# A two-group decoder trunk: weight low parts in two GpSimd operations, and a subtraction of the channel mixer one flush later

## The chip, the cores and the metric

The kernel runs on one core of one Trainium2 chip. The metric is the device time of one execution in microseconds (us), the median of several runs. The engines are called as in the profile: PE is TensorE (matrix products), DVE is VectorE, ACT is ScalarE, POOL is GpSimd, SP is the queue that issues the transfers. "L153" is line 153 of the kernel.

## The reference

One inference step of a decoder of two layers, for two groups of tokens that share one set of weights: a prompt of 1024 tokens and a sample group of 8 sequences with 8 new tokens each (64 tokens, with 1024 cached positions). The width is 1024, the channel mixer's hidden width 2816, everything is float32.

```python
def swiglu(h, w_in, w_out):
    g, u = jnp.split(h @ w_in, 2, axis=-1)
    return (jax.nn.silu(g) * u) @ w_out

for layer in range(DEPTH):
    hn = rms_norm(h, norm_mix_g[layer])
    if layer % 2 == 0:      # convolution module + stick-breaking attention, one in- and one out-projection
        mix = conformer_sb_mixer(hn, ...)
    else:                   # short gated convolution + causal pooling
        mix = shortconv_pool_mixer(hn, ...)
    h = h + mix
    h = h + swiglu(rms_norm(h, norm_ffn_g[layer]), w_ffn_in[layer], w_ffn_out[layer])
y = rms_norm(h, norm_final_g)
```

Outputs are y for both groups, the new keys and values, and the new states of the convolutions and the pooling.

## The kernel before, in words

**High and low parts.** Each float32 operand of a matrix product is used as two numbers: a high part, which is the operand copied to the matrix format, and a low part, which is the operand minus its high part. A product is made of three (`mm3`, L167 to L171): high weight by high operand, high weight by low operand, low weight by high operand, in this order for each 128 rows of the contraction. All run under line L170.

**Weights.** The weights come in 278 tiles of 128 x 1024 numbers, in one fixed list (`seq`). A tile of an input projection holds eight blocks of 128 contraction rows by 128 outputs; a tile of the channel mixer's second matrix holds two blocks of rows by 512 outputs. `w_load` has SP fetch a tile into one of three `stage` buffers. `w_split` has ACT copy the high part (L152) and POOL subtract for the low part (L153) into one of three `hl` buffers. `w_next` hands out a tile, splits those up to two ahead and loads up to five ahead. So the split of a tile waits on ACT until TensorE is done with the tile three before it, and POOL waits for ACT.

**Queues.** The order of instructions on each engine is the order in which the program writes them; only semaphores between engines hold them back. Work that evicts a block of products can leave a second part behind in the list `post`; `flush` runs what the list holds, and the program calls it behind the products of a later block, so that on every engine those instructions stand there.

**The stages.** Tokens are worked in two groups for the first layer, GA (tokens 0 to 511, one block of 512 columns) and GB (512 to 1087, two blocks of 288), and all together in the second, GT (1088 in three blocks of 364, 364 and 360). First come the input projections of both groups, with convolution and attention of GA between their blocks (`bg` and `slot` run one piece of such work at a time). Then the output projection (`run_out`) and channel mixer (`run_ffn`) of GA, with attention of GB, sample attention, convolution and its norm (`conv_norm`) between the blocks; then output projection and channel mixer of GB; then the second layer.

**The channel mixer** (`run_ffn`) works hidden blocks of 128 in pairs: for a pair q it makes a gate block and a value block for f = 2q and for f = 2q + 1 (`one`), 24 products for each block of columns. Behind the products of each such block it flushes, then evicts. The gate's eviction (`ev_g`) multiplies by the norm factor on DVE (L226) and applies the gate: for GA a sigmoid on ACT (L363) and a product on POOL (L364), for GB and GT one function on ACT (L366). The value's eviction (`ev_u`) does L226 and posts `fin`: the gated product on POOL (L378), then `split`: the high part on ACT (L175) and the low part on DVE (L176), into the tile `hid`. Then come the eight output products of the pair before (`out_block`, six products for each block of columns), each evicted by an addition on DVE (`added`, L230) into the residual stream `hb`. A flush stands behind the second of the eight. TensorE has three accumulators for GA and GB and two for GT. At the end (q = 11) there is one more flush, and the function `last` makes the eight output products of the last pair. For GA, `last_a` puts in front of each L230 the split of an operand of the output projection that follows (`mix_operand`, also L175 and L176, tile `x`); for GB, `to_mixer` adds squares (L183, L186, L187) and prepares the next operands (L304, L307); for GT, `to_y` makes the final output (products L1385, additions L1388).

**Temporaries.** All of these take their scratch tiles from one pool (`tmp`): four buffers of 640 columns in the first layer, three of 1152 in the second. The value block's scratch is read by L378, L175 and L176. Sample attention (L1020) and the convolution's norm (L186, L748) take from it as well.

Lines named later: L194 and L218 are the products of a norm, L502 to L530 feed the input, L781, L784, L815, L818 and L820 are DVE's steps of the attention, L830 transposes its weights, L722 and L729 to L750 are the convolution's norm, L931 and L932 split transposed keys of the sample attention, and L1000 and L1001 transpose its weights.

Of the kernel before, what the change touches and what calls it, by code (L numbers as in the profile page):

```python
# [11 lines left out]
AF = mybir.ActivationFunctionType  # L12
OP = mybir.AluOpType
# [16 lines left out]
def f32(ap):  # L30
    return ap.bitcast(F)
# [27 lines left out]
def trunk_kernel(ctx, tc, x_prompt, x_sample, cache_k, cache_v, state_conformer, state_shortconv, state_pool,  # L59
# [4 lines left out]
    pe, act, dve, pool, sp = nc.tensor, nc.scalar, nc.vector, nc.gpsimd, nc.sync  # L64
# [11 lines left out]
    def tmp():  # L76
        return tmpbox[0].tile([128, tmpbox[1]], F, name="tmp")
# [60 lines left out]
    def w_load(upto):  # L138
        while nxt[0] < min(upto, len(seq)):
            i = nxt[0]  # L140
            src, kt = seq[i]
            stage[i] = wpool.tile([128, 1024], F, name="stage", bufs=3)
            sp.dma_start(stage[i].rearrange("p (k n) -> p k n", k=kt), src)
            nxt[0] += 1

    def w_split(upto):
        while nxt[1] < min(upto, len(seq)):
            i = nxt[1]
            w_load(i + 1)
            st = stage.pop(i)  # L150
            hl = wpool.tile([128, 2, 1024], FR, name="hl", bufs=3)
            act.activation(hl[:, 0], st, AF.Copy)  # L152
            pool.tensor_tensor(hl[:, 1], st, f32(hl[:, 0]), op=OP.subtract)  # L153
            hls[i] = hl.rearrange("p s (k n) -> p s k n", k=seq[i][1])
            nxt[1] += 1

# [2 lines left out]
    def w_next(live=0):  # L159
        j = wj[0]  # L160
        wj[0] += 1
        w_split(j + 3 - live)
        w_load(j + 6 - live)
        return hls.pop(j)
# [8 lines left out]
    def split(dst, src, g=None):  # L173
        if g is None:
            act.activation(dst[:, 0], src, AF.Copy)  # L175
            dve.tensor_tensor(dst[:, 1], src, f32(dst[:, 0]), op=OP.subtract)  # L176
        else:
            act.activation(dst[:, 0], src, AF.Copy, scale=g)
            dve.scalar_tensor_tensor(dst[:, 1], src, g, f32(dst[:, 0]), op0=OP.mult, op1=OP.subtract)
# [44 lines left out]
    def scaled(g, dst, acc):  # L224
        for a, d, r in parts(g, acc, dst, rr[:, g.cs]):
            dve.tensor_tensor(d, a, r, op=OP.mult)  # L226

    def added(g, dst, acc):
        for a, d in parts(g, acc, dst):
            dve.tensor_tensor(d, a, d, op=OP.add)  # L230

    post = []

    def flush():
        todo = post[:]
        post.clear()
        for f in todo:
            f()

    K0 = list(range(KC))  # L240
# [2 lines left out]
    def block(g, a, h, x, ks=K0, mid=None, slot=None):  # L243
        for i, k in enumerate(ks):
            if i == 4 and mid:
                mid()
            if slot and i in (2, 4, 6):
                slot()
            mm3(g, a, h[:, 0, k], h[:, 1, k], x[k], k == ks[0], k == ks[-1])
# [30 lines left out]
    def run_in(g, accs, x, evacs, hooks, ks=K0, tail=(lambda: None,) * 2):  # L280
        a0, a1 = pair(g, accs, x, K0, hooks)
        evacs[0](a0)
        evacs[1](a1)
        for i, e in enumerate(evacs[2:]):
            h = w_next()
            a = accs()
            end = i == len(evacs) - 3
            block(g, a, h, x, ks if end else K0, flush)
            if end:
                tail[0]()  # L290
            e(a)
            if end:
                tail[1]()
        flush()
# [44 lines left out]
    def norm_hooks(g, ps, count=D, at=(4, 6)):  # L339
        box = {}  # L340

        def fa():
            box["d"] = norm_a(g, ps, count)

        return {at[0]: [fa], at[1]: [lambda: norm_b(g, ps, box["d"])]}

    def out_block(g, a, h, i, hh):
        for k in range(2):
            mm3(g, a, h[:, 0, k, i * 128:i * 128 + 128], h[:, 1, k, i * 128:i * 128 + 128], hh[:, k], k == 0, k == 1)


    def run_ffn(g, accs, ps, hidp, x, last, sig=False, slot=lambda: None):
        G = NF // 2
        n = g.n
        hid = {}
        gate = {}

        def ev_g(a):
            t = tmp()
            scaled(g, t[:, :n], a)  # L360
            if sig:
                s = tmp()
                act.activation(s[:, :n], t[:, :n], AF.Sigmoid)  # L363
                pool.tensor_tensor(t[:, :n], t[:, :n], s[:, :n], op=OP.mult)  # L364
            else:
                act.activation(t[:, :n], t[:, :n], AF.Silu)  # L366
            gate["t"] = t

        def ev_u(f, a):
            if f // 2 not in hid:  # L370
                hid[f // 2] = hidp.tile([128, 2, 2, n], FR, name="hid")
            dst = hid[f // 2][:, f % 2]
            t = tmp()
            scaled(g, t[:, :n], a)
            u = gate.pop("t")

            def fin():
                pool.tensor_tensor(t[:, :n], t[:, :n], u[:, :n], op=OP.mult)  # L378
                split(dst, t[:, :n])
            post.append(fin)  # L380

        def one(f, which):
            h = w_next()
            a = accs()
            block(g, a, h, x, slot=slot)
            flush()
            ev_g(a) if which == 0 else ev_u(f, a)
            slot()

        for q in range(G + 1):  # L390
            if q < G:
                for f in (2 * q, 2 * q + 1):
                    if f == 0:
                        run_in(g, accs, x, [ev_g, lambda a: ev_u(0, a)], norm_hooks(g, ps))
                        slot()
                        continue
                    one(f, 0)
                    one(f, 1)
            if q == G:
                flush()  # L400
                last(hid.pop(q - 1))
            elif q:
                hh = hid.pop(q - 1)
                for o in range(2):
                    h = w_next()
                    for i in range(4):
                        a = accs()
                        out_block(g, a, h, i, hh)
                        added(g, hb[:, o * 4 + i, g.cs], a)
                        if o == 0 and i == 1:  # L410
                            flush()
                        slot()
# [51 lines left out]
    def accs():  # L464
        return accbox["p"].tile([128, len(accbox["g"].blocks), 512], F, name="acc")
# [12 lines left out]
    st = ststack.enter_context(tc.tile_pool(name="start", bufs=1, side="right"))  # L478
# [701 lines left out]
    def last_a(hh):  # L1180
        drain()
        for o in range(2):
            h = w_next()
            for i in range(4):
# [5 lines left out]
                sp.dma_start(park[:, n, GA.cs], hb[:, n, GA.cs])  # L1190

    run_ffn(GA, accs, ms, hidp, x1, last_a, sig=True, slot=bg)
    hstack.close()

# [33 lines left out]
    with tc.tile_pool(name="hid0b", bufs=2) as hidp:  # L1228
        run_ffn(GB, accs, ms, hidp, x1, to_mixer, slot=slot_d)
# [245 lines left out]
```

## Time and profile before

| what | us |
|---|---|
| median of 3 runs | 2708.38 |
| lowest and highest | 2707.59, 2709.07 |
| the profiled execution's own time | 2708.54 |
| its span in the profile | 2706.8 |
| PE busy in it | 2603.3 |
| L153 (278 operations of POOL) busy | 679.5 |
| L176 into `hid` (66 operations of DVE) | 28.4, 16.7 and 15.6 for GT, GB and GA |

The page and the views come from one profiled execution. Busy time is what an engine's instructions lasted. A view of waits gives, for an engine and line, how long the engine sat idle before it and which instruction ended that wait. A timeline gives start, length, engine, line, operation, output and inputs, and in brackets the idle time before and its releaser; a row may merge neighbouring instructions of one kind ("x3"). TensorE's products overlap, so its gaps and its rate in a long run say more than the length of one product.

### The profile page before, as it was taken

What the parts mean: (1) busy time and instruction counts of PE and PEld (TensorE: products, weight loads), DVE (VectorE), ACT (ScalarE), POOL (GpSimd) and SP (SyncE); (2) the same over time, 40 slices, a digit from 0 to 9 for tenths busy, and PEclk for the clock granted to TensorE, in tenths of its full rate; (3) what the DMA queues carried; (4) which work ended last, traced back from release to release, by engine and by line L of the source; (5) the groups of instructions that cost most, each with busy time, mean ns of one, the idle gap of its engine ahead of it and who ended that gap; (6) DMA issues with size and microseconds to landing.
All of it is one profiled execution on the core that took longest, in us unless ns stands there. A gap on an engine that the chain in (4) does not pass through costs nothing. (4 is left out here: it accounts for less than half of the span.)

```text
span 2706.8 us, 37823 instructions
## 1 busy us (share of the span) xinstructions
PE 2603.3 (96%) x15423; PEld 2365.3 (87%) x15423; DVE 1212.3 (45%) x1730; ACT 868.3 (32%) x1326; POOL 1031.1 (38%) x589
## 2 busy tenths in 40 slices
PE   8989998998999998999999989999999999999997
PEld 6788876887666656899999989999999999999997
DVE  4774776868677642322222243343122222222226
ACT  4436765653433323332222232132211111111112
POOL 5655243343333337464444442224222222222222
PEclk9999999999999999999999999999999999999999
DMA  6432231234444432422222221131111111111111
GB/s 198 123 96 78 66 99 40 62 90 133 144 137 146 120 110 70 136 86 86 79 86 87 79 91 47 43 106 47 39 48 39 47 47 40 48 47 40 47 39 67
DMA packets 293380, 218.75 MB, mean 81 GB/s; under 512 B 21505, under 2 KB 248961, under 8 KB 293192
## 3 DMA queue, kind: packets, MB, share of 16 engines
q1 hardware_dynamic: 293176, 216.33, 26.8%
q8 instruction: 122, 2.00, 0.3%
q14 instruction: 50, 0.41, 0.1%
q10 hardware_dynamic: 32, 0.01, 0.0%
HBM read 198.09 MB, written 18.69 MB: 80 GB/s over the span
## 5 line engine op out<-in xcount | busy, mean ns | idle before, releaser
L153 POOL TENSOR_TENSOR hl<-stage,hl 128x1024 fp32r<-128x1024 f32 x278 | 679.5, 2446 | 1209.9 <-ACT hl L152 816.6
L170 PE MATMUL acc<-x1t,hl 128*128 128x364 f32 (+1 forms) x4896 | 824.1, 330 | 7.1 <-DVE hb L230 6.5
L170 PEld LDWEIGHTS acc<-x1t,hl 128*128 128x128 f32 x4896 | 817.2, 189 | 9.2 <-ACT x1t L304 6.7
L170 PE MATMUL acc<-x,hl 128*128 128x288 f32 (+1 forms) x4704 | 804.3, 325 | 12.9 <-DVE hb L230 9.6
L170 PEld LDWEIGHTS acc<-x,hl 128*128 128x128 f32 x4704 | 690.8, 189 | 88.7 <-issue 39.6
L170 PE MATMUL acc<-hid,hl 128*128 128x364 f32 (+2 forms) x3024 | 530.4, 333 | 20.5 <-DVE hb L230 17.5
L170 PEld LDWEIGHTS acc<-hid,hl 128*128 128x128 f32 x3024 | 480.0, 190 | 58.4 <-DVE hb L230 23.2
L152 ACT ACTIVATE hl<-stage 128x1024 fp32r<-128x1024 f32 x278 | 292.1, 1054 | 585.9 <-PE acc L170 318.5
L226 DVE TENSOR_TENSOR tmp<-acc,rr 128x728 f32<-128x728 f32 (+2 forms) x230 | 160.6, 720 | 684.3 <-PE acc L170 681.6
L230 DVE TENSOR_TENSOR hb<-acc,hb 128x728 f32<-128x728 f32 (+2 forms) x368 | 255.3, 720 | 273.2 <-PE acc L170 272.2
L176 DVE TENSOR_TENSOR hid<-tmp,hid 128x512 fp32r<-128x512 f32 (+2 forms) x66 | 60.8, 921 | 201.8 <-ACT hid L175 201.6
L187 POOL TENSOR_TENSOR ss<-ss,tmp 128x512 f32<-128x512 f32 (+2 forms) x55 | 98.4, 1789 | 91.6 <-ACT tmp L186 89.3
L378 POOL TENSOR_TENSOR tmp<-tmp 128x512 f32<-128x512 f32 (+2 forms) x66 | 117.1, 1774 | 29.3 <-ACT tmp L366 28.2
L175 ACT ACTIVATE hid<-tmp 128x512 fp32r<-128x512 f32 (+2 forms) x66 | 53.4, 809 | 230.8 <-POOL tmp L378 230.8
L170 PE MATMUL acc<-x1a,hl 128*128 128x512 f32 x480 | 122.4, 408 | 3.7 <-POOL hl L153 2.3
L366 ACT ACTIVATE tmp<-tmp 128x576 f32<-128x576 f32 (+1 forms) x44 | 39.6, 900 | 256.1 <-DVE tmp L226 256.1
L170 PEld LDWEIGHTS acc<-x1a,hl 128*128 128x128 f32 x480 | 89.9, 191 | 27.1 <-POOL hl L153 3.8
L693 DVE SCALAR_TENSOR_TENSOR cacc<-ext,par,cacc 128x512 f32<-128x512 f32 x120 | 90.1, 751 | 2.3
L364 POOL TENSOR_TENSOR tmp<-tmp 128x512 f32<-128x512 f32 x22 | 31.7, 1439 | 120.3 <-ACT tmp L363 113.1
L839 PE MATMUL o<-wt,vrow 128*64 128x128 f32 x576 | 76.6, 278 | 0.4 <-ACT wt L831 0.4
L818 DVE TENSOR_TENSOR_SCAN q<-q,ones 128x384 f32<-128x384 f32 (+6 forms) x56 | 76.0, 1357 | 2.0
L655 DVE SCALAR_TENSOR_TENSOR cacc<-ext,par,cacc 128x512 f32<-128x512 f32 x100 | 75.4, 754 | 3.0
(222 smaller groups left out, 1880.2 us busy)
## 6 DMA issues: line engine op xcount, KB each, us to landing
stage<-in_w_ffn_in_dram SPq DMA_DIRECT2D x132, 512.0 KB
stage<-in_w_ffn_out_dram SPq DMA_DIRECT2D x66, 512.0 KB
stage<-in_w_in_even_dram SPq DMA_DIRECT2D x40, 512.0 KB
kst<-in_cache_k_dram SPq DMA_DIRECT2D x64, 256.0 KB
vst<-in_cache_v_dram SPq DMA_DIRECT2D x64, 256.0 KB
stage<-in_w_out_even_dram SPq DMA_DIRECT2D x16, 512.0 KB
stage<-in_w_in_odd_dram SPq DMA_DIRECT2D x16, 512.0 KB
park<-hb SPq DMA_DIRECT2D x16, 288.0 KB
```

Source lines behind the costliest of these rows:

```text
L152: act.activation(hl[:, 0], st, AF.Copy)
L153: pool.tensor_tensor(hl[:, 1], st, f32(hl[:, 0]), op=OP.subtract)
L170: pe.matmul(acc[:, b, :c1 - c0], w, x[:, xi, c0:c1], start=first and s == 0, stop=last and s == 2)
L176: dve.tensor_tensor(dst[:, 1], src, f32(dst[:, 0]), op=OP.subtract)
L187: pool.tensor_tensor(ss[:, g.cs], ss[:, g.cs], t[:, :g.n], op=OP.add)
L226: dve.tensor_tensor(d, a, r, op=OP.mult)
L230: dve.tensor_tensor(d, a, d, op=OP.add)
L378: pool.tensor_tensor(t[:, :n], t[:, :n], u[:, :n], op=OP.mult)
L655: dve.scalar_tensor_tensor(acc, i, w, acc, op0=OP.mult, op1=OP.add)
L693: dve.scalar_tensor_tensor(o, i, w, o, op0=OP.mult, op1=OP.add)
L818: dve.tensor_tensor_scan(e, e, ones[:, 0:1].to_broadcast([128, n - 128]), q[:, n - 128:n - 127], op0=OP.mult, op1=OP.mult)
L839: pe.matmul(o, vrow[h][:, j], w[:, j], start=j == 0, stop=j == i)
```

## The change

Two edits. In `w_split`, the subtraction of a weight tile's low part becomes two operations on POOL, one for columns 0 to 511 and one for 512 to 1023. For a tile of an input projection these are contraction blocks 0 to 3 and 4 to 7, for a tile of the second matrix the first and the second contraction block.

In the channel mixer, `fin` no longer calls `split`: POOL's product and ACT's copy stay in `fin`, and DVE's subtraction goes to a new list `late`. `flush` takes both lists as they stand at its start and runs `post` first, then `late`; so a subtraction that `fin` adds runs in the next flush. At the end of a channel mixer `flush` is called twice.

```diff
             act.activation(hl[:, 0], st, AF.Copy)
-            pool.tensor_tensor(hl[:, 1], st, f32(hl[:, 0]), op=OP.subtract)
+            for c in (slice(0, 512), slice(512, 1024)):
+                pool.tensor_tensor(hl[:, 1, c], st[:, c], f32(hl[:, 0, c]), op=OP.subtract)
...
     post = []
 
+    late = []
+
     def flush():
-        todo = post[:]
+        todo, low_parts = post[:], late[:]
         post.clear()
-        for f in todo:
+        late.clear()
+        for f in todo + low_parts:
             f()
...
             def fin():
                 pool.tensor_tensor(t[:, :n], t[:, :n], u[:, :n], op=OP.mult)
-                split(dst, t[:, :n])
+                act.activation(dst[:, 0], t[:, :n], AF.Copy)
+                late.append(lambda: dve.tensor_tensor(dst[:, 1], t[:, :n], f32(dst[:, 0]), op=OP.subtract))
             post.append(fin)
...
             if q == G:
+                flush()
                 flush()
                 last(hid.pop(q - 1))
```

## The prediction

> **What bounds the kernel now.** I read the page first, then the busy time by stage, then the waits, and then the timeline wherever TensorE stood still.
>
> ```profile
> PE 2603.3 (96%) x15423; PEld 2365.3 (87%) x15423; DVE 1212.3 (45%) x1730; ACT 868.3 (32%) x1326; POOL 1031.1 (38%) x589
> ```
>
> TensorE is busy for 2603.3 of 2706.8 us, so no edit that only moves work between the other engines can win more than the 103.5 us in which it idles. The view by stage says where that idle time lies. Its columns are the stretch, its length, then busy time and count of PE, weight loads, DVE, ACT and POOL.
>
> ```profile
> 350.00:464.00 114.00, 102.93 (x554) 83.08 (x554) 89.98 (x86) 73.95 (x114) 42.60 (x33) 0.96 0.25 71
> 464.00:1085.00 621.00, 583.45 (x2674) 423.88 (x2672) 404.01 (x635) 255.59 (x469) 245.06 (x146) 0.98 0.37 111
> ...
> 1220.00:1570.00 350.00, 349.75 (x2653) 349.52 (x2652) 102.63 (x135) 89.07 (x101) 161.49 (x76) 1.00 0.29 87
> ...
> 1900.00:2657.00 757.00, 755.89 (x4530) 754.18 (x4530) 198.07 (x277) 116.20 (x112) 206.52 (x85) 1.00 0.14 43
> ```
>
> The first channel mixer (464 to 1085) leaves TensorE idle for 37.6 us, the other two (1220 to 1570, 1900 to 2657) for 0.3 and 1.1 us. So two of the three mixer passes cannot get faster at all. What the change wins must come from the first 1100 us, where attention and convolution run between the mixer's blocks.
>
> The moved subtraction (L176) is the end of a chain over three engines: product on POOL (L378), copy on ACT (L175), subtraction on DVE. The view of waits shows DVE standing at it:
>
> ```profile
> ACT hid L175 <- POOL tmp L378: 230.8, 55, 8.1
> DVE hid L176 <- ACT hid L175: 201.6, 46, 11.4
> ```
>
> Those 201.6 us matter only where something that TensorE needs is queued behind L176 on DVE. The timeline at the end of the first channel mixer has two such places, one in each of these groups of rows (start, length, engine, line; the bracket gives the idle time before and what ended it):
>
> ```profile
> 1058.51 0.63 ACT L175 ACTIVATE hid<-tmp 128x512 fp32r<-128x512 f32 x1 [5.34 <-POOL tmp L378]
> 1059.17 0.69 DVE L176 TENSOR_TENSOR hid<-tmp,hid 128x512 fp32r<-128x512 f32 x1 [11.43 <-ACT hid L175]
> 1059.78 0.68 DVE L226 TENSOR_TENSOR tmp<-acc,rr 128x512 f32<-128x512 f32 x1
> 1060.50 0.63 ACT L363 ACTIVATE tmp<-tmp 128x512 f32<-128x512 f32 x1 [1.36 <-DVE tmp L226]
> ...
> 1061.27 1.28 POOL L364 TENSOR_TENSOR tmp<-tmp 128x512 f32<-128x512 f32 x1 [2.80 <-ACT tmp L363]
> ...
> 1062.59 0.69 DVE L226 TENSOR_TENSOR tmp<-acc,rr 128x512 f32<-128x512 f32 x1 [2.12 <-POOL tmp L364]
> ...
> 1063.33 3.54 PE L170 MATMUL acc<-hid,hl 128*128 128x512 f32 x14 [1.15 <-DVE tmp L226]
> ...
> 1071.28 1.26 POOL L378 TENSOR_TENSOR tmp<-tmp 128x512 f32<-128x512 f32 x1
> 1072.58 0.63 ACT L175 ACTIVATE hid<-tmp 128x512 fp32r<-128x512 f32 x1 [5.89 <-POOL tmp L378]
> 1073.12 1.04 ACT L152 ACTIVATE hl<-stage 128x1024 fp32r<-128x1024 f32 x1
> 1073.24 0.69 DVE L176 TENSOR_TENSOR hid<-tmp,hid 128x512 fp32r<-128x512 f32 x1 [8.77 <-ACT hid L175]
> 1073.85 1.88 DVE L230 TENSOR_TENSOR hb<-acc,hb 128x512 f32<-128x512 f32 x3
> ...
> 1074.59 10.70 PE L170 MATMUL acc<-hid,hl 128*128 128x512 f32 x36 [5.68 <-DVE hb L230]
> ```
>
> At 1073.85 three additions (L230) leave DVE in a row: their products had been ready, L176 stood ahead of them, and TensorE, with three accumulators, had none left for 5.68 us. An earlier pass has the same picture with 4.38 us:
>
> ```profile
> 1025.67 1.21 DVE L176 TENSOR_TENSOR hid<-tmp,hid 128x512 fp32r<-128x512 f32 x1 [5.99 <-ACT hid L175]
> ...
> 1027.54 6.01 PE L170 MATMUL acc<-hid,hl 128*128 128x512 f32 x18 [4.38 <-DVE hb L230]
> ...
> 1033.21 1.43 POOL L187 TENSOR_TENSOR ss<-ss,tmp 128x576 f32<-128x576 f32 x1
> ```
>
> **Part 1: L176 one flush later.** No instruction is added, and no DMA moves with it. In each step the subtraction of the odd block leaves its place behind the second of the eight output products and lands behind the next gate block, past six L230 on DVE; that of the even block moves from behind the next gate block to behind the next value block, past one L226. Its input is long there by then. POOL's and ACT's parts stay where they are, so ACT's own waits for POOL stay too.
>
> *The end of the first mixer.* At 1059 the gate's eviction (L226) no longer stands behind L176, so the sigmoid (L363) starts when ACT is done with L175, at 1059.14 and not at 1060.50: 1.36 us, which L364, the second L226 and the products at 1063.33 inherit. At 1073 the three L230 leave at once, and the 5.68 us go. So does the slow restart: 36 products in 10.70 us are 0.297 us each, against
>
> ```profile
> 1042.51 15.64 PE L170 MATMUL acc<-x,hl 128*128 128x512 f32 x66
> ...
> 1082.79 2.56 DVE L176 TENSOR_TENSOR x<-hb,x 128x576 fp32r<-128x576 f32 x1 [0.97 <-ACT x L175]
> ...
> 1096.59 3.67 PE L170 MATMUL acc<-x,hl 128*128 128x288 f32 x26 [2.23 <-DVE hb L230]
> ```
>
> 0.237 us in a long run, so 36 x 0.060 = 2.2 us. Together 9.2 us at most. What is late next: the last pass itself. Its first output product needs the low part of the last block, which now follows all eight L230 on DVE; by the chain of L378, L175 and L176, moved up by 1.36, that is ready near 1073.0, while TensorE would ask for it near 1071.6 (a wait of 1.4). Behind that, eight pairs of operand subtraction (L176, another tile) and L230 on DVE run from 1082.79 until 1096.5. They can start once ACT, free of L175 near 1072.3, has made two weight copies of 1.04 and one operand copy: near 1075.3 (an estimate), seven us earlier, and with more of POOL's work falling into them they would end five to six us earlier. I take 5.5 us, with 2 and 9 as bounds.
>
> *The pass at 1027.* The wait and the slow restart (6.01 for 18 products, 4.27 in a long run) are 6.1 us. But the norm of the second token group follows in TensorE's queue and needs the last addition of squares on POOL, which ends at 1033.21 + 1.43 = 1034.64. In the trace TensorE comes to it 18 products after 1033.39 (4.36 us), at about 1037.6. So at most 3 us come through, and a colder restart takes some of it. I take 2 us (bounds 1 and 3).
>
> *The ends of the other two mixers.* Here L176 comes behind the last L230, and the last pass asks for its result at once.
>
> ```profile
> L176 DVE TENSOR_TENSOR hid<-tmp,hid 128x1088 fp32r<-128x1088 f32 x22 | 28.4, 1293 | 70.1 <-ACT hid L175 70.1
> ...
> L176 DVE TENSOR_TENSOR hid<-tmp,hid 128x576 fp32r<-128x576 f32 x22 | 16.7, 758 | 77.8 <-ACT hid L175 77.8
> ```
>
> ```profile
> 1555.81 12.51 PE L170 MATMUL acc<-hid,hl 128*128 128x288 f32 x95
> ...
> 1557.44 0.76 DVE L230 TENSOR_TENSOR hb<-acc,hb 128x576 f32<-128x576 f32 x1 [0.80 <-PE acc L170]
> ```
>
> ```profile
> 2657.57 1.66 PE L1385 MATMUL blk<-hid,hl 128*128 128x384 f32 x8 [1.54 <-DVE hb L230]
> ```
>
> At 1557.44 this L230 starts about 0.2 after its product; 0.76 for it and 0.76 for L176 end at 1558.96. TensorE can do eight products of 0.13 us (12.51 / 95) without the low part, to about 1558.3, and waits 0.7. At 2657.57 four products of 0.21 us (1.66 / 8) go ahead, to 2658.4, and L176 ends 1.29 after the same L230, near 2658.8: 0.4. Sum: a loss of 1.1 us (bounds 0.5 and 1.5).
>
> **Part 2: L153 in two operations.** The columns are busy time, mean of one, idle before:
>
> ```profile
> L153 POOL TENSOR_TENSOR hl<-stage,hl 128x1024 fp32r<-128x1024 f32 x278 | 679.5, 2446 | 1209.9 <-ACT hl L152 816.6 <-issue 330.2 <-PE m L928 21.2
> ...
> L378 POOL TENSOR_TENSOR tmp<-tmp 128x512 f32<-128x512 f32 x22 | 29.8, 1357 | 1.1 <-DVE tmp L226 0.9
> ```
>
> No row shows the new shape. The nearest is L378 with 512 columns: 1.26 us undisturbed (1071.28), so two make 2.52 against 2.39, and POOL gets 278 x 0.13 = 36 us more, at most 278 x (2 x 1.357 - 2.446) = 75. POOL idles for 1676 us, mostly for ACT, which is the cover; it is gone only where TensorE waits for a chain through POOL. I charge 0.5 us (0 to 2.5) for those.
>
> What it gives comes from two sides. First, products of the low weights wait for their own half only:
>
> ```profile
> PE acc L170 <- POOL hl L153: 4.7, 4, 1.5
> ```
>
> Four waits, 4.7 us, one of them inside the handover costed above; a first half is ready about 1.2 us earlier. The two at the start lie in a stage paced by loads. I take 2 us (0 to 4.4).
>
> Second, DVE. A DVE operation with two operands in SBUF stands still while POOL works:
>
> ```profile
> 439.41 5.09 POOL L153 TENSOR_TENSOR hl<-stage,hl 128x1024 fp32r<-128x1024 f32 x2 [0.86 <-ACT hl L152]
> 439.50 5.55 DVE L781 TENSOR_TENSOR kt<-kall,kt 64x512 fp32r<-64x512 f32 x2
> ...
> 445.91 1.62 PE L170 MATMUL acc<-x,hl 128*128 128x512 f32 x3 [7.38 <-DVE hb L230]
> ```
>
> Two L781 take 5.55 us beside two L153, in turn: each gets in when one L153 ends. With halves they get in after the first and the second half, near 440.6 and 442.3, and L230 starts about 2.1 us earlier. Another such pair:
>
> ```profile
> PE m L830 <- DVE be L820: 5.1, 3, 3.5
> ```
>
> ```profile
> 468.36 6.07 POOL L153 TENSOR_TENSOR hl<-stage,hl 128x1024 fp32r<-128x1024 f32 x2 [2.81 <-ACT hl L152]
> ...
> 469.16 3.05 DVE L820 TENSOR_TENSOR be<-be,q 128x895 f32<-128x895 f32 x1
> ```
>
> L820 would start its work when the first half ends, 1.2 us sooner; for the three waits together up to 2.8 us. Where several two-operand operations follow one another, the second half catches the next one and nothing is won. So 4 us, with 0 and 6 as bounds.
>
> The Trainium skill, "SBUF — State Buffer", section "SBUF: two separate sides", says that the shared port pair is an exclusive lock held for the whole instruction, the first comer winning. By that rule alone the second half could also win every time against DVE, and the 4 us would be 0. The strict turns at 439 to 445 speak against that.
>
> The Trainium skill, "TensorE: Matmul & The Clock Gate", section "What's actually happening", puts the slow clock behind an idle window of about 3.4 us. The wait at 445.91, cut from 7.38 to about 5.3, would stay over it, so by that rule no restart is saved there. The trace agrees that long waits are followed by slow products (0.297 us after 5.68).
>
> **Sum.** -5.5 - 2 + 1.1 + 0.5 - 2 - 4 = -11.9 us against the profiled execution's 2708.54 (its span of 2706.8 and 1.74 around it). The median of the runs shown, 2708.38, is 0.16 lower, so the forecast is 2708.38 - 11.9 = 2696.5. All terms at their good ends give -9 - 3 + 0.5 - 4.4 - 6 = -21.9 (2686.5); all at their bad ends -2 - 1 + 1.5 + 2.5 = +1 (2709.4).
>
> **The rivals.** *The gain is given back.* POOL paces the stretch from 1010 to 1080, and a TensorE that runs ahead only meets the next POOL result earlier. For it: L187 at 1033.21. Against it: the 5.68 us wait ends on L176 and not on POOL's backlog. Time: 2708.4 - 3 = 2705, within 0.2% (5.4 us, about what a measurement of this kernel can tell from no change). Chance 0.21.
>
> *A temporary held too long (slower).* The product's temporary is now read one flush later, in a pool of four that the gate, the sigmoid, the sample attention and the convolution's norm share. Where the next sigmoid (L363) or a norm piece gets that buffer, ACT waits for L176, and everything behind it on ACT with it: key copies and attention weights that TensorE needs. The row at 1062.59 shows the pool tight already (DVE waits 2.12 for L364). Price: up to a gate block, 24 x 0.237 = 5.7 us, less what hides it, some 3 us. It decides from the sixth occurrence in the 22 blocks: six lose 18, and with the 11.9 the time is 2714.5. Against it: a plain block takes three temporaries, so the buffer normally comes round two blocks later. Chance 0.09.
>
> *More than costed.* Shorter DVE stalls keep the clock up elsewhere and all bounds fall well: 2687. Chance 0.08.
>
> *The change does not separate the halves*: the products still wait for both. Then the 2 us of the first side go, 2698.5; it lies in my range and is counted in the forecast.
>
> **How the numbers follow.** Forecast, 2690 to 2702: 0.62. The range reaches from the case of more than costed into that within 0.2%, 2687 to 2708, near the sums of the bounds. Faster by over 0.2% is below 2703: 0.62 + 0.08 = 0.70. Within 0.2%: 0.21. Slower: 0.09.
>
> **What would show it.** Right: in 464 to 1097 TensorE waits for L230 only briefly, the waits at 1027 and 1074 are gone, L176 of the gated block no longer waits for L175, L153 has 556 operations of about 1.27 us, L781 beside L153 takes under 2 us. The stages from 1100 on keep their lengths but for 0.7 and 0.4 us at the two ends. Wrong: an ACT wait for DVE L176 before L363, a wait of TensorE for hid's L176 of over 2 us, or 1033 as a new wait of L194 for POOL that swallows the gain.

## The result and the profile after

| kernel | median us | lowest to highest | ratio to before |
|---|---|---|---|
| before | 2708.48 | 2707.59 to 2709.07 | |
| changed | 2690.37 | 2687.58 to 2692.77 | 0.9933 [0.9916, 0.9950] |

The change takes 18.1 us off, against 11.9 forecast. The profiled execution of the changed kernel took 2689.21 us, its span is 2687.4. In the new text, lines after L152 stand one further down (L171 are the products, L227 the norm factor, L231 the additions of DVE, L188 the sums of squares, L195 the norm's products), L154 is the halved subtraction of the weights, L382 POOL's gated product, L383 its copy on ACT and L384 the deferred subtraction on DVE; the attention's steps L815, L818, L820 and L830 are now L821, L824, L826 and L836.

From the profile page of the changed kernel, busy time and the costliest groups:

```profile
PE 2603.0 (97%) x15423; PEld 2365.1 (88%) x15423; DVE 1198.2 (45%) x1730; ACT 867.4 (32%) x1326; POOL 1095.7 (41%) x867
...
L154 POOL TENSOR_TENSOR hl<-stage,hl 128x512 fp32r<-128x512 f32 x556 | 746.3, 1365 | 1157.4 <-issue 597.6
...
L383 ACT ACTIVATE hid<-tmp 128x512 fp32r<-128x512 f32 (+2 forms) x66 | 53.4, 809 | 238.6 <-POOL tmp L382 238.4
...
L384 DVE TENSOR_TENSOR hid<-tmp,hid 128x512 fp32r<-128x512 f32 (+2 forms) x66 | 70.7, 1071 | 18.1 <-ACT hid L383 18.0
```

TensorE does the same 2603 us of work, so the gain is idle time. DVE's 201.6 us of waiting ahead of the gated subtraction are down to 18.0, while ACT's wait for POOL (230.8 before, 238.4 now) stays: the deferral moved only DVE's part. POOL has 746.3 - 679.5 = 66.8 us more of L154, inside the 36 to 75 forecast; one half takes 1.365 us on the mean, not 1.27.

The view of waits for TensorE (us in total, times, longest):

```profile
PE acc L171 <- DVE hb L231: 19.1, 8, 5.2
PE m L1006 <- ACT wts L1007: 9.1, 4, 3.4
...
PE m L836 <- DVE be L826: 3.8, 5, 1.4
...
PE m L195 <- POOL ss L188: 2.5, 2, 1.7
...
PE acc L171 <- POOL hl L154: 2.1, 3, 1.3
```

The first row was 33.6 us, the waits of the attention's transposes for DVE 9.5, those for low weights (L153) 4.7. The row of L195 is new: the norm that was forecast to be late next.

To say where the time went, I compare the start of the same product of TensorE in two traces (all kernels issue the same 15423 in the same order). The stretches are cut at products that start at 452, 484, 1020, 1041 and 1100 us in the kernel before. Each number is what a stretch of that kernel is longer (+) or shorter (-) than in the kernel before, in us; the last column stops a few products before the end. The kernels below the first row are those of the experiments. Each row is one profiled execution, the medians are of several.

| kernel | to 452 | 452-484 | 484-1020 | 1020-1041 | 1041-1100 | from 1100 | sum |
|---|---|---|---|---|---|---|---|
| changed | -4.3 | -4.1 | -2.5 | -2.7 | -7.2 | +2.0 | -18.8 |
| split only | -3.8 | -2.3 | -2.2 | +0.8 | +0.8 | -0.4 | -7.1 |
| late only | -0.2 | -4.0 | +0.3 | -3.5 | -6.6 | +2.3 | -11.6 |
| second half first | -2.7 | -4.1 | -2.7 | -2.7 | -7.2 | +2.2 | -17.1 |
| late for GA only | -3.1 | -4.1 | +1.0 | -2.7 | -7.2 | -0.4 | -16.4 |
| late, odd blocks only | -4.6 | -2.2 | -0.6 | +0.1 | -6.4 | +2.5 | -11.3 |
| late, even blocks only | -3.2 | -4.1 | -3.2 | -0.2 | -1.3 | -0.7 | -12.7 |
| four parts | -2.4 | -3.6 | -2.0 | -3.4 | -8.4 | +5.3 | -14.4 |
| copy late too | -3.8 | -6.8 | -5.3 | -5.1 | -5.9 | -0.4 | -27.2 |
| copy late, not for the last pair | -4.9 | -6.8 | -6.7 | -3.5 | -7.2 | -0.5 | -29.6 |
| changed, again | -5.8 | -4.1 | -2.6 | -2.7 | -7.2 | +1.9 | -20.5 |

The first and the last row are one kernel: from 452 on they agree to 0.2 us, before that, where transfers pace the start, they differ by 1.5. "Late for GA only" issues the same work in the same order until the end of the first mixer and yet differs by 3.5 us in 484 to 1020. So differences of one to three us between kernels in that column, and of one or two in the first, are put down to no edit here. In the last column, too, two rows hold something that the edit does not explain by itself: behind the first norm after 1100 (near 1140) TensorE's granted clock halved for some products in the odd kernel, which is about 1.5 of its +2.5, and in the kernel of four parts, about 3 of its +5.3.

### The profile page after: what moved, and what is told of

Same layout as the page of the kernel before. It is cut to its first block, busy times and chain, and to the rows that moved or that the text cites. A ratio compares the mean times of both kernels' runs of the same rounds, so it can differ in the third digit from the quotient of the medians.

```text
span 2687.4 us, 38206 instructions
## 1 busy us (share of the span) xinstructions
PE 2603.0 (97%) x15423; PEld 2365.1 (88%) x15423; DVE 1198.2 (45%) x1730; ACT 867.4 (32%) x1326; POOL 1095.7 (41%) x867
## 5 line engine op out<-in xcount | busy, mean ns | idle before, releaser
L154 POOL TENSOR_TENSOR hl<-stage,hl 128x512 fp32r<-128x512 f32 x556 | 746.3, 1365 | 1157.4 <-issue 597.6
L171 PE MATMUL acc<-x1t,hl 128*128 128x364 f32 (+1 forms) x4896 | 824.2, 330 | 5.9 <-DVE hb L231 5.2
L171 PEld LDWEIGHTS acc<-x1t,hl 128*128 128x128 f32 x4896 | 817.3, 190 | 8.0 <-ACT x1t L308 5.4
L171 PE MATMUL acc<-x,hl 128*128 128x288 f32 (+1 forms) x4704 | 807.1, 326 | 9.6 <-DVE hb L231 7.5
L171 PEld LDWEIGHTS acc<-x,hl 128*128 128x128 f32 x4704 | 693.5, 190 | 85.6 <-issue 34.8
L171 PE MATMUL acc<-hid,hl 128*128 128x364 f32 (+2 forms) x3024 | 527.3, 332 | 9.0 <-DVE hb L231 6.4
L171 PEld LDWEIGHTS acc<-hid,hl 128*128 128x128 f32 x3024 | 477.0, 189 | 47.0 <-DVE hb L231 12.9
L227 DVE TENSOR_TENSOR tmp<-acc,rr 128x728 f32<-128x728 f32 (+2 forms) x230 | 160.7, 721 | 795.5 <-PE acc L171 788.2
L152 ACT ACTIVATE hl<-stage 128x1024 fp32r<-128x1024 f32 x278 | 292.0, 1054 | 576.5 <-PE acc L171 422.4
L231 DVE TENSOR_TENSOR hb<-acc,hb 128x728 f32<-128x728 f32 (+2 forms) x368 | 257.3, 720 | 318.5 <-PE acc L171 317.7
L188 POOL TENSOR_TENSOR ss<-ss,tmp 128x512 f32<-128x512 f32 (+2 forms) x55 | 97.0, 1763 | 82.5 <-ACT tmp L187 81.6
L383 ACT ACTIVATE hid<-tmp 128x512 fp32r<-128x512 f32 (+2 forms) x66 | 53.4, 809 | 238.6 <-POOL tmp L382 238.4
L382 POOL TENSOR_TENSOR tmp<-tmp 128x512 f32<-128x512 f32 (+2 forms) x66 | 117.1, 1775 | 28.1 <-ACT tmp L370 27.1
L171 PE MATMUL acc<-x1a,hl 128*128 128x512 f32 x480 | 122.2, 408 | 2.6 <-POOL hl L154 1.3
L171 PEld LDWEIGHTS acc<-x1a,hl 128*128 128x128 f32 x480 | 89.9, 192 | 25.8 <-POOL hl L154 2.9
L699 DVE SCALAR_TENSOR_TENSOR cacc<-ext,par,cacc 128x512 f32<-128x512 f32 x120 | 90.0, 750 | 2.3
L824 DVE TENSOR_TENSOR_SCAN q<-q,ones 128x384 f32<-128x384 f32 (+6 forms) x56 | 81.4, 1453 | 2.0
L938 DVE TENSOR_TENSOR kth<-m,kth 128x384 fp32r<-128x384 f32 (+1 forms) x96 | 48.3, 508 | 68.5 <-ACT kth L937 68.5
L384 DVE TENSOR_TENSOR hid<-tmp,hid 128x512 fp32r<-128x512 f32 (+2 forms) x66 | 70.7, 1071 | 18.1 <-ACT hid L383 18.0
L845 PEld LDWEIGHTS o<-wt,vrow 128*64 128x64 f32 x576 | 61.2, 136 | 19.0 <-issue 8.2
```

What stands on the lines that cost most here:

```text
L154: pool.tensor_tensor(hl[:, 1, c], st[:, c], f32(hl[:, 0, c]), op=OP.subtract)
L171: pe.matmul(acc[:, b, :c1 - c0], w, x[:, xi, c0:c1], start=first and s == 0, stop=last and s == 2)
L188: pool.tensor_tensor(ss[:, g.cs], ss[:, g.cs], t[:, :g.n], op=OP.add)
L383: act.activation(dst[:, 0], t[:, :n], AF.Copy)
L384: late.append(lambda: dve.tensor_tensor(dst[:, 1], t[:, :n], f32(dst[:, 0]), op=OP.subtract))
L699: dve.scalar_tensor_tensor(o, i, w, o, op0=OP.mult, op1=OP.add)
```

## The experiments

The kernel before ran beside them at 2708.3 (first four), 2708.6 (next four) and 2708.3 us (last two).

**Split only**: the kernel before with the two operations of POOL and nothing else.

```diff
-            pool.tensor_tensor(hl[:, 1], st, f32(hl[:, 0]), op=OP.subtract)
+            for c in (slice(0, 512), slice(512, 1024)):
+                pool.tensor_tensor(hl[:, 1, c], st[:, c], f32(hl[:, 0, c]), op=OP.subtract)
```

> Only the two POOL operations, the subtraction of the gated block where it was. Comparing the start of each TensorE product before and after the change, the changed kernel gained 1.3 us up to 30 us of the span, 2.2 at the addition behind L781 (445), 4.1 around 467 to 480, 1.7 at 523 and 548, lost 2.5 between 680 and 800, gained 2.8 at 965 and 10.7 between 1005 and 1097, and 1.0 at 1150. Theory 'two places' (the deferral makes the gains at 467 and 1005 to 1097, the split the others): 6 to 8 us faster than before, near 2701, with the waits of 4.4 and 5.7 us at 1027 and 1074 still there. Theory 'lock' (shorter POOL operations free DVE, and that alone is most of it): 12 us or more faster, near 2695, and the waits at 1027 and 1074 much shorter. Theory 'POOL pays' (36 to 67 us more POOL work eats it): within 2 us of before.

Measured: 2700.6 (2698.9 to 2701.8), ratio 0.9969 [0.9957, 0.9981], -7.7 us. That is the first theory's 6 to 8, and the two long waits for DVE's additions at the end of the first mixer are still there (4.65 and 6.51 us in its profile).

**Late only**: the changed kernel with one operation for a weight tile.

```diff
-            for c in (slice(0, 512), slice(512, 1024)):
-                pool.tensor_tensor(hl[:, 1, c], st[:, c], f32(hl[:, 0, c]), op=OP.subtract)
+            pool.tensor_tensor(hl[:, 1], st, f32(hl[:, 0]), op=OP.subtract)
```

> Only the later subtraction, each weight tile's low part in one POOL operation. 'Two places': about 12 us faster than before, near 2696: 4 around 467, 9 to 10 between 1005 and 1097, less 1 to 2 at the ends of the second and third mixer; the 7.4 us wait at 445 stays. 'Lock': 2 to 6 us faster, near 2704, because DVE still stands behind whole POOL operations when the additions come. If the two edits help each other, the two gains together fall short of the 18 us of both at once by 3 us or more; if they add, they meet it within 2.

Measured: 2696.3 (2695.0 to 2697.9), ratio 0.9955 [0.9941, 0.9969], -12.0 us. The two parts alone make 19.7, together 18.1. By the table the deferral alone wins in 452-484 and 1020-1100 and nothing elsewhere; the split alone wins before 1020 and loses 1.6 us behind it. Both overlap in 452-484: 2.3 and 4.0 alone, 4.1 together. The gains add up within 2 us. So the deferral is the larger part, and the split is no pure cost.

**Second half first**: the changed kernel makes columns 512 to 1023 ahead of 0 to 511, so that the products that come first wait for both halves.

```diff
-            for c in (slice(0, 512), slice(512, 1024)):
+            for c in (slice(512, 1024), slice(0, 512)):
```

> The changed kernel with the two POOL operations in the other order: columns 512 to 1023 first. The products of the first contraction blocks then wait for the later operation, and DVE sees the same two short operations. If the gains at the start and at 1150 come from products that wait for their own half only, they go: 2 to 3 us slower than the changed kernel, near 2693, with PE waits for hl L154 of 4 to 5 us in sum as before the change. If they come from DVE being freed sooner, the time is the changed kernel's within 1 us, near 2690.

Measured: 2690.3 (2688.1 to 2694.3), ratio 0.9932 [0.9919, 0.9946]: the same as the changed kernel, although TensorE's waits for low weights are back at 5.4 us (2.1 in the changed kernel, 4.7 before). That the first half is ready earlier brings nothing that the medians show. One such place suggests why. The kernel before waited 1.53 us for low weights at 1150, and the kernel with the second half first 1.77; the changed kernel waits 0.54, and then 0.77 at the next norm for POOL's squares, where the other two do not stop:

```profile
1128.69 6.87 PE L171 MATMUL acc<-x,hl 128*128 128x288 f32 x50 [0.54 <-POOL hl L154]
1136.33 1.28 PE L195 MATMUL m<-ones,ss 128*128 128x1 f32 x10 [0.77 <-POOL ss L188]
```

**Late for GA only**: the other two mixers subtract at once again.

```diff
-                late.append(lambda: dve.tensor_tensor(dst[:, 1], t[:, :n], f32(dst[:, 0]), op=OP.subtract))
+                low_part = lambda: dve.tensor_tensor(dst[:, 1], t[:, :n], f32(dst[:, 0]), op=OP.subtract)
+                late.append(low_part) if g is GA else low_part()
```

> The changed kernel with the later subtraction in the first mixer pass (GA) alone; in the other two it stands where it stood before. 'Two places' says that the deferral brings nothing there and costs 0.5 us at the end of the second pass and 0.2 to 1.8 at the end of the third: 0.7 to 2.3 us faster than the changed kernel, near 2689, and the row of blk products at 2637 starts without a wait for hid L384. If the deferral also helps in the other two passes, it is slower than the changed kernel.

Measured: 2689.1 (2685.8 to 2692.2), ratio 0.9924 [0.9910, 0.9937]; from the changed kernel it cannot be told apart by the medians. Its profile shows the price of the two ends: the last column goes from +2.0 to -0.4.

**Odd blocks only, even blocks only**: the subtraction of every second hidden block goes back to its place.

```diff
-                late.append(lambda: dve.tensor_tensor(dst[:, 1], t[:, :n], f32(dst[:, 0]), op=OP.subtract))
+                low_part = lambda: dve.tensor_tensor(dst[:, 1], t[:, :n], f32(dst[:, 0]), op=OP.subtract)
+                late.append(low_part) if f % 2 == 1 else low_part()    # the other kernel: == 0
```

> Weights in two operations; only the subtraction of odd hidden blocks (f = 2q + 1) runs a flush later, that of even blocks stays in its place. Theory of places (the gain lies at four spots, each with the block whose subtraction stands ahead of what TensorE needs): the two waits of the first mixer's end, at 1027 and 1074, belong to odd blocks and stay gone (about 9 us together), the ones near 467 and 1059 belong to even blocks and come back (some 3 to 4 us), the ends of the three mixers still pay about 2 us: 3 to 4 us slower than the changed kernel, 2694. Rival (the subtraction blocks DVE everywhere a little, so that half of the deferrals give half of the gain of 12 us): 6 us slower, 2696.5.

> The counterpart: only the subtraction of even hidden blocks runs a flush later. Theory of places: the waits at 1027 and 1074 come back (about 9 us), the ends of the three mixers pay nothing (2 us back), the gain near 467 stays: 6 to 8 us slower than the changed kernel, 2697. Rival of half and half: 6 us slower too, but then the odd and the even run give the same; by the theory of places they differ by 3 to 4 us, and the profile shows DVE's three additions in a row behind the subtraction again near 1027 and 1074.

Measured: odd 2697.5 (2694.5 to 2700.0), ratio 0.9959 [0.9945, 0.9972]; even 2695.5 (2694.4 to 2696.4), ratio 0.9951 [0.9938, 0.9965]. Both missed what the theory of places said (2694 and 2697), and it had the odd kernel ahead, while the even one is faster by 2.0 us, with overlapping intervals. So the medians lie on the side of half and half: from split only they win 3.1 and 5.1, of 10.2 with both. But the stretches do not halve. With even blocks alone the end of the mixer shows the old picture (timeline of that kernel):

```profile
1061.63 0.69 DVE L384 TENSOR_TENSOR hid<-tmp,hid 128x512 fp32r<-128x512 f32 x1 [9.09 <-ACT hid L383]
1062.24 1.88 DVE L231 TENSOR_TENSOR hb<-acc,hb 128x512 f32<-128x512 f32 x3
1062.98 4.41 PE L171 MATMUL acc<-hid,hl 128*128 128x512 f32 x12 [6.51 <-DVE hb L231]
```

Three additions leave in a row behind the subtraction, and 1041-1100 wins 1.3 us; with odd blocks alone it wins 6.4 of 7.2. So the wait at 1074 belongs to the odd block, as said. What was wrong is the pass at 1027. Odd blocks alone win 6.2 us there by 1033, and by 1041 all of it is lost at the norm (timeline of the odd kernel, TensorE and POOL):

```profile
1011.77 8.10 PE L171 MATMUL acc<-hid,hl 128*128 128x512 f32 x34
1019.70 4.36 PE L171 MATMUL acc<-x,hl 128*128 128x512 f32 x18
1027.27 2.29 PE L195 MATMUL m<-ones,ss 128*128 128x1 f32 x10 [3.21 <-POOL ss L188]
```

```profile
1025.79 1.42 POOL L188 TENSOR_TENSOR ss<-ss,tmp 128x576 f32<-128x576 f32 x1
```

TensorE stands 3.21 us for the squares that POOL ends at 1027.2. The rest of the loss is slow products behind it: the granted clock is 0.57 in 1026 to 1034, and the next 12 products take 4.81 us, for 3.05 in the kernel before. In the changed kernel, with even blocks late as well, that wait is 1.69. Here, and near 467, the even blocks bring the rest.

**Four parts**: weights in four operations of 256 columns.

```diff
-            for c in (slice(0, 512), slice(512, 1024)):
+            for c in (slice(0, 256), slice(256, 512), slice(512, 768), slice(768, 1024)):
```

> The changed kernel with the low weights in four operations of 256 columns. Theory of turns (POOL and DVE alternate one operation each, so a shorter POOL operation only helps where one or two DVE operations stand against one weight tile): nothing more or little, and POOL busy 50 to 100 us longer by its fixed cost per operation, which goes to chains that TensorE waits for: 2690 to 2693. Rival (the time for which DVE is locked out per POOL operation sets what is lost, so that halving it again gives a second time what the halves gave, 6 us): 2685.

Measured: 2694.2 (2691.4 to 2696.5), ratio 0.9946 [0.9932, 0.9959], 3.8 us above the changed kernel (the intervals of the two ratios overlap; the changed kernel measured again, below, gave 2690.6), and a little above what either theory said. Its page, and two places on its timeline:

```profile
L154 POOL TENSOR_TENSOR hl<-stage,hl 128x256 fp32r<-128x256 f32 x1112 | 850.8, 797 | 1097.7 <-issue 571.9
```

```profile
375.11 5.17 POOL L154 TENSOR_TENSOR hl<-stage,hl 128x256 fp32r<-128x256 f32 x4
380.23 0.13 POOL L814 MEMSET be<- 128x1 f32 x2
...
380.38 0.47 PE L836 MATMUL m<-ident,be 128*128 128x128 f32 x1 [2.81 <-POOL be L814]
...
1137.93 2.12 PE L195 MATMUL m<-ones,ss 128*128 128x1 f32 x10 [1.87 <-POOL ss L188]
1139.91 5.70 PE L171 MATMUL acc<-x,hl 128*128 128x288 f32 x24
```

POOL is busy 104.5 us longer in L154 (0.797 us a part), and at 375 a memset of the attention stands behind four parts that take 5.17 us between DVE's operations; TensorE waits 2.81 us for it (1.44 for DVE at that product in the changed kernel). The largest loss is at 1138: TensorE waits 1.87 us for POOL's squares, 0.77 in the changed kernel, and the 24 products behind take 5.70 us, 3.42 there, at a granted clock of 0.57 in 1138 to 1146. So shorter operations of POOL help DVE (below) and hurt POOL's own chain. That four parts are worse than two is likely from the medians; how much of it is POOL's time and how much the clock is not separated.

**Copy late too**: for GA, ACT's copy goes to the later flush with DVE's subtraction; for GB and GT neither is late.

```diff
-                act.activation(dst[:, 0], t[:, :n], AF.Copy)
-                late.append(lambda: dve.tensor_tensor(dst[:, 1], t[:, :n], f32(dst[:, 0]), op=OP.subtract))
+                def parts_of():
+                    act.activation(dst[:, 0], t[:, :n], AF.Copy)
+                    dve.tensor_tensor(dst[:, 1], t[:, :n], f32(dst[:, 0]), op=OP.subtract)
+                late.append(parts_of) if g is GA else parts_of()
```

> The changed kernel, but for the first group ACT's copy of the gated block goes a flush later as well, with DVE's subtraction behind it; for the other two mixers copy and subtraction both stand in the earlier flush, as in the kernel before. If ACT's wait for POOL's gated product (238 us in the profile, which the change left in place) holds up attention weights and key copies that TensorE needs, that wait is gone and the time falls by 4 to 9 us below the changed kernel: 2682 to 2686, with fewer waits of the attention's transposes for ACT between 464 and 1000. If that wait only fills idle time of ACT, the time stays at 2688 to 2690 (the ends of the second and third mixer give back 2 us, the last pass of the first mixer gets its high part later and costs up to 1).

Measured: 2681.5 (2679.3 to 2687.7), ratio 0.9905 [0.9890, 0.9920], 8.9 us below the changed kernel. From "late for GA only" it differs by GA's copy alone, and is 7.6 us below that; by the table 2.4 of the gain over the changed kernel is at the ends of the other two mixers, which are not late here. The timeline of the changed kernel at one of four waits for attention weights, and then the same place with the copy late (its L1010 and L1009 are the L1007 and L1006 of the changed kernel):

```profile
881.05 0.63 ACT L383 ACTIVATE hid<-tmp 128x512 fp32r<-128x512 f32 x1 [0.97 <-POOL tmp L382]
881.70 1.29 ACT L1007 ACTIVATE wts<-m 128x512 f32<-128x512 f32 x3
...
882.35 0.14 PEld L1006 LDWEIGHTS m<-ident,wx 128*128 128x128 f32 x1 [3.65 <-ACT wts L1007]
```

```profile
878.33 1.29 ACT L1010 ACTIVATE wts<-m 128x512 f32<-128x512 f32 x3
...
878.98 0.14 PEld L1009 LDWEIGHTS m<-ident,wx 128*128 128x128 f32 x1 [2.53 <-ACT wts L1010]
```

ACT stood 0.97 us for POOL and then made the copy, with the weights for TensorE behind it; without that TensorE waits 1.1 us less. At 464 it is 1.76 us, which goes altogether. So ACT's wait, which the change left and to which the forecast gave no price, did hold TensorE up.

The same kernel has one new wait, at the last pair of blocks: pieces of the convolution's norm stand ahead of the copy on ACT, and subtraction, L227 and TensorE wait in a chain (its L385 and L386 are copy and subtraction):

```profile
1043.18 0.61 ACT L385 ACTIVATE hid<-tmp 128x512 fp32r<-128x512 f32 x1
...
1043.90 0.71 DVE L386 TENSOR_TENSOR hid<-tmp,hid 128x512 fp32r<-128x512 f32 x1 [10.86 <-ACT hid L385]
1044.53 0.68 DVE L227 TENSOR_TENSOR tmp<-acc,rr 128x512 f32<-128x512 f32 x1
...
1045.26 10.89 PE L171 MATMUL acc<-hid,hl 128*128 128x512 f32 x40 [5.14 <-DVE tmp L227]
```

**Copy late, but not for the last pair** (against the kernel above; `high` and `low` are its copy and its subtraction, each as a function of its own, not shown):

```diff
-                late.append(parts_of) if g is GA else parts_of()
+                if g is GA and f < 20:
+                    late.extend([high, low])      # ACT's copy, DVE's subtraction
+                else:
+                    high()
+                    late.append(low) if g is GA else low()
```

> As the run with the copy deferred too, but for the last pair of hidden blocks (f = 20 and 21) ACT's copy goes back into the earlier flush, only DVE's subtraction stays late. Theory: there the copy of block 20 stood behind the norm pieces of the convolution on ACT, DVE's subtraction and the gate's eviction L227 behind it, and TensorE waited 5.14 us at 1045; with the copy moved back that wait shrinks to about 0.6 (as in the changed kernel at 1048) and 3 to 5 us are won: 2677 to 2679. Rival (the handover behind it is paced by POOL's weight halves and DVE's pairs, which start no earlier, so that the wait only moves to 1070): 2681, as without it.

Measured: 2682.0 (2679.2 to 2683.0), ratio 0.9902 [0.9887, 0.9917]: as without it; the 3 to 5 us did not come. The wait of 5.14 is 0.57, as expected, but the rival holds for the larger part (timeline of DVE, then of TensorE):

```profile
1052.38 1.69 DVE L177 TENSOR_TENSOR x<-hb,x 128x576 fp32r<-128x576 f32 x1 [1.78 <-ACT x L176]
...
1065.07 0.68 DVE L231 TENSOR_TENSOR hb<-acc,hb 128x512 f32<-128x512 f32 x1
```

```profile
1039.59 4.26 PE L171 MATMUL acc<-hid,hl 128*128 128x512 f32 x17 [0.57 <-DVE tmp L227]
...
1065.90 2.45 PE L171 MATMUL acc<-x,hl 128*128 128x288 f32 x10 [2.23 <-DVE hb L231]
```

DVE's eight pairs of operand subtraction and addition last from 1052.38 to 1065.75, 13.4 us as in the changed kernel, and TensorE meets them earlier and waits more between them. By the starts of the products, the shorter wait put TensorE 5.9 us further ahead of the kernel above; it lost 3.1 of that among the pairs, and 1.5 behind them, where the granted clock is 0.86 in 1066 to 1078 (1.00 at that place without the edit). Another 1.5 it had lost ahead of that wait, at the norm. In the medians nothing remains, nor in the stretches that the edit can reach: from 1020 to 1100 the two kernels have -11.0 and -10.7. The 2.4 us between their sums lie ahead of that.

**Changed, again**: no edit.

> The changed kernel once more, with nothing altered, beside the run before on the same chip. If the several us between profiles of identical code are the spread of executions, its median comes out within 2 us of 2690.4 and its profile differs from the earlier one by steps of 1 to 2 us in both directions in the first 1100 us. If they belong to the kernels, this profile repeats the earlier one to within 0.5 us throughout.

Measured: 2690.6 (2687.5 to 2692.6), ratio 0.9933 [0.9919, 0.9947]. The median repeats within 0.3 us. Neither expectation fits the profile as a whole: up to 452 us it moves by 1.5, behind that it repeats to 0.2. What the 3.5 us of "late for GA only" come from stays open. Its profile is of its longest execution (2692.2, the others from 2685.8), and the two of the changed kernel are of shorter ones (2689.2 and 2687.5, the others up to 2692.8); so the scatter of one kernel's executions is neither shown to be it nor ruled out.

## Why the prediction was right, and what it mis-sized

The sign, the place (the first 1100 us) and the range of 2687 to 2708 hold, and the two handovers of the first mixer went as described. The forecast is 6.2 us short. Its terms for the split, +0.5, -2 and -4, make -5.5 against -7.7 measured alone; its terms for the deferral, -5.5, -2 and +1.1, make -6.4 against -12.0. So 5.6 us were missing in the deferral and 2.2 in the split, less 1.6 that the two do not win together.

*The end of the first mixer*, -5.5 forecast: -7.2, or -6.6 with the deferral alone. Both waits behind the subtraction are gone, and what is late next is what was named: a short wait for the last block's parts, then DVE's pairs (changed kernel, DVE and TensorE).

```profile
1058.31 0.69 DVE L384 TENSOR_TENSOR hid<-tmp,hid 128x512 fp32r<-128x512 f32 x1 [0.36 <-ACT hid L383]
1058.33 0.50 PE L171 MATMUL acc<-hid,hl 128*128 128x512 f32 x1 [0.42 <-ACT hid L383]
1059.06 3.53 PE L171 MATMUL acc<-hid,hl 128*128 128x512 f32 x14 [0.22 <-DVE hid L384]
1060.78 1.69 DVE L177 TENSOR_TENSOR x<-hb,x 128x576 fp32r<-128x576 f32 x1 [1.77 <-ACT x L176]
...
1073.46 0.68 DVE L231 TENSOR_TENSOR hb<-acc,hb 128x512 f32<-128x512 f32 x1
1074.28 4.13 PE L171 MATMUL acc<-x,hl 128*128 128x288 f32 x18 [2.23 <-DVE hb L231]
```

The waits of 0.42 and 0.22 stand for the 1.4 forecast. The pairs last 13.4 us, and the 2.23 behind them is to the hundredth that at 1096.59 before.

*The pass at 1027*, -2: -2.7 in 1020-1041, inside its bounds of 1 and 3 (-3.5 with the deferral alone). The eight products of the pair run without a stop and the norm takes part of it back (changed kernel):

```profile
1020.89 1.43 POOL L188 TENSOR_TENSOR ss<-ss,tmp 128x576 f32<-128x576 f32 x1
...
1022.38 1.27 PE L195 MATMUL m<-ones,ss 128*128 128x1 f32 x10 [1.69 <-POOL ss L188]
```

Here the rival that the gain is given back is right, for this pass alone; with odd blocks alone it is wholly right.

*The step that failed* is the reading that only the end of the first mixer and the pass at 1027 have something behind the subtraction that TensorE needs. There is a third place, ahead of both, which I put down to the lock between POOL and DVE, that is, to DVE operations standing still while POOL works (before):

```profile
465.59 0.63 ACT L175 ACTIVATE hid<-tmp 128x512 fp32r<-128x512 f32 x1 [2.76 <-POOL tmp L378]
...
466.25 0.69 DVE L176 TENSOR_TENSOR hid<-tmp,hid 128x512 fp32r<-128x512 f32 x1 [4.72 <-ACT hid L175]
...
466.86 0.42 DVE L815 TENSOR_TENSOR_SCAN q<-q,ident 128x128 f32<-128x128 f32 x1
...
472.36 1.73 PE L830 MATMUL m<-ident,be 128*128 128x128 f32 x7 [3.49 <-DVE be L820]
```

The attention's scans L815 and L818 and the step L820 stood behind L176, which waited 4.72 us for ACT. I quoted the last wait and L820's 3.05 us beside POOL, and did not look at what DVE had done before. In the changed kernel the subtraction comes at 472.46, the step at 459.48:

```profile
459.48 2.00 DVE L826 TENSOR_TENSOR be<-be,q 128x895 f32<-128x895 f32 x1
462.65 0.63 ACT L383 ACTIVATE hid<-tmp 128x512 fp32r<-128x512 f32 x1 [4.08 <-POOL tmp L382]
...
463.97 1.96 PE L845 MATMUL o<-wt,vrow 128*64 128x128 f32 x16 [1.76 <-ACT wt L837]
```

That is -4.0 us in 452-484 with the deferral alone; the split alone wins 2.3 there, so the lock had a part, but the two together win no more than 4.1. The last row is where the next wait of that chain stands, ACT's for POOL; the copy made late took it.

*The two later ends*, +1.1: by the starts of the same products +0.8 at the second, as forecast 0.7, and +2.0 at the third, forecast 0.4. The wait for the low part was there, and short; the products behind it ran slowly (changed kernel; then the stretch, with the granted clock third from the end):

```profile
2636.78 0.93 PE L1391 MATMUL blk<-hid,hl 128*128 128x384 f32 x4 [1.54 <-DVE hb L231]
2637.88 4.27 PE L1391 MATMUL blk<-hid,hl 128*128 128x384 f32 x14 [0.17 <-DVE hid L384]
```

```profile
2636.00:2642.00 6.00, 5.05 (x19) 4.72 (x20) 2.94 (x5) 1.04 (x2) 0.16 (x1) 0.72 0.00 1
```

14 products in 4.27 us at a clock of 0.72; with odd blocks alone, behind the same waits of 1.54 and 0.17, the same 14 took 2.70 at a clock of 1.00, and that end cost 0.4.

*POOL's extra*, +0.5: not seen by itself. Split only loses 1.6 us in 1020-1100, where no loss was named, and that lies within the bounds of 0 and 2.5; whether POOL's 66.8 us cause it is not shown.

*Own half only*, -2: waits for low weights fell from 4.7 to 2.1, so the halves are told apart; but with their order turned round they are 5.4, and the time is the same: no gain that the medians show.

*DVE freed*, -4: at 445.91 it is the forecast 2.1 (5.22 for 7.38, changed kernel):

```profile
437.24 5.85 POOL L154 TENSOR_TENSOR hl<-stage,hl 128x512 fp32r<-128x512 f32 x4 [0.86 <-ACT hl L152]
437.33 3.40 DVE L787 TENSOR_TENSOR kt<-kall,kt 64x512 fp32r<-64x512 f32 x2
...
441.59 6.59 PE L171 MATMUL acc<-x,hl 128*128 128x512 f32 x17 [5.22 <-DVE hb L231]
```

The attention's waits for DVE went from 9.5 to 6.1 with the split alone, that is 3.4 less, against the up to 2.8 taken for them.

*The slower rival*, a temporary held too long, did not happen: no sigmoid L367 waits for L384.

## What to carry to other kernels

A wait on one engine is harmless only until the next instruction in its queue that the busiest engine needs; so go through every place where the moved instruction stands and look at what is queued behind it, also where the profile names another instruction as the one that ended the wait. When the last link of a chain over three engines is moved later, move the middle one as well: here ACT's copy in the first mixer was worth 7.6 us more. Price a removed wait only up to the next thing that paces the stretch, here the sums of squares on POOL and eight pairs on DVE, which, with slow products behind the waits, took back 6 us of a gain of 6 in one kernel and the 3 to 5 expected in another.

## What the runs showed of the hardware that I had not expected

POOL and DVE take turns by the instruction, and a shorter POOL instruction shortens each turn but makes more of them. For every DVE operation I took its length over the shortest of its line and shape, and added up what is over 0.2 us and lies beside a weight subtraction, an estimate from the traces: 99.9 us in 69 operations before, 81.2 in 102 with the split only; 114.5 in 79 with the deferral only, 86.6 in 107 in the changed kernel, 62.8 in 150 with quarters. Halving POOL's operation cuts the single turn from 1.45 to 0.80 us (99.9 / 69, 81.2 / 102), but the sum by only a fifth to a quarter.

The Trainium skill, "SBUF — State Buffer", section "SBUF: two separate sides", gives the lock to whichever starts first, for a whole instruction; the second part agrees, and at 437 to 441 above DVE got in between the halves, so that POOL did not win every turn, as it could have by that rule alone.

The clock can halve after less idle time than I had allowed for, and not always. In the changed kernel it was 0.50 from 2638.22 to 2641.63, and in the 3.41 us before that TensorE had been busy for 1.70, with the two waits of 1.54 and 0.17 us; in the odd kernel it was 1.00 behind the same two waits. Near 1140 it is the other way round: behind waits of 0.54 and 0.77 us the next 24 products took 3.42 us in the changed kernel, behind 0.53 and 0.76 us they took 4.87 in the odd one. The Trainium skill, "TensorE: Matmul & The Clock Gate", section "What's actually happening", puts the slow clock behind an idle window of about 3.4 us that runs freely; the runs show a dependence on the moment, but no idle time of that length here.
